# A third place for output weights' parts, filled by adding DMAs two tiles ahead, and more projection steps before attention's first scores

## The chip, the cores and the metric

The kernel runs on one core of a Trainium2 chip. Its metric is the time of one execution on the device in microseconds (us). The time before is the median of three runs, 1197.37 us (1196.95 to 1198.57). One further look comes from the hardware profiler, which recorded one execution instruction by instruction.

Five engines work side by side: TensorE (PE, matmuls; the loading of its weights is listed as PEld), VectorE (DVE), ScalarE (ACT), GpSimd (POOL) and SyncE (SP, which here only issues DMAs). Each works through its own queue in order and waits there for semaphores.

## The reference

One layer of an encoder block on 1024 tokens of width 1024, in float32. The parts that matter here:

```python
n = rmsnorm(h, ln_g)
proj = n @ w_in                       # q, k, v of both head groups
y_na  = neighbourhood_attention(...)  # 8 heads of 64
y_gla = bidirectional_gla(...)        # gated linear attention, 4 heads
h = h + concat([y_na, y_gla]) @ w_out
h = h + square(relu(rmsnorm(h) @ w1)) @ w2
out = rmsnorm(h)
```

All matmuls are made to float32 accuracy from two parts: every operand x is held as a high part (x rounded to the matmul's type) and a low part (x minus the high part). A product takes three matmuls: high by high, high by low, low by high.

## The kernel before, in words

The program is written for a planner. It emits instructions in program order with priorities; the planner fixes the order on each engine, gives tiles their memory and sets the semaphores. A block under `tc.high_priority(offset=n)` is treated as if it had been emitted n places earlier. `tc.keep_in_program_order` fixes an instruction's order among all instructions of its engine that are so marked; all matmuls and transposes are.

**Weights' parts.** `weights(block, eng)` loads a block of 128 by 1024 weights (512 KB) with SP into a tile wf and makes its two parts. With an engine given, `split` lets ACT round wf into wh, and that engine (DVE, called V, or POOL, called G) subtracts: wl = wf - wh. Without one, ACT writes wl = -(wf rounded), POOL issues a DMA which adds the block from memory to wl, and ACT writes wh. wf, wh and wl have two places each in the pool stg: six places of 4 KB per partition, 24 KB in all. The blocks of the input projection go the second way, one block ahead; the blocks of w_out go the first way.

**Attention.** While the attention of one pair of heads runs, the input projection of the next pair fills TensorE's gaps. A list of generators (`Fill`) holds the projections; one step of it is three matmuls (three parts' products for one of eight blocks of the contraction), a half of a block is eight steps, and after each half DVE evacuates the bank. `NA_PRE` steps run before the first scores. Then pairs p = 0 to 3 run over blocks b = 0 to 7; the table `NA_FILL[p][b]` says how many steps stand before the next block's scores (`softmax`), before the current block's turn (`turn`, transposes of the scaled scores) and after it. The projection of a pair's values is followed by transposes of its own, which are held back until `NA_LATE` further steps have run, or until they are needed. `softmax` uses the two banks "s": two products per head, then DVE adds the bias (L804), ACT takes the exponential (L806), DVE scales (L809). `turn` and the value transposes share the two banks "t" (for the last pair's values, "mm"). ACT copies out the high part (L834, L774), DVE subtracts the low one (L835, L775). The first pair's bias is finished by DVE at L749. In pair 3, after block 2, no projection steps are left; from there on the list holds the first half's output tiles.

**Output projection.** The tokens have two halves of 512. For each half there are eight output tiles d of 128 rows; a tile takes 8 blocks of the contraction times three matmuls, 24 in all (`sums`), into a bank "mm", and DVE adds the bank to hT (L716). The first half's tiles run beside the last attention blocks without the last block of the contraction, which follows in eight short products (`opl`) from parts of their own (wk). The second half's tiles (hf = 1) run after it: tile 0, the eight short products, tiles 1 to 7. Each tile's parts are asked for where the tile is emitted, by `split` on DVE for d = 1 to 3 and on POOL for d = 4 to 7. `ff_in` squares each tile on ACT (L932) and sums the squares, on POOL for the first half and on DVE for the second (L934). After tile 2 of the second half, the first half is normed: DVE writes nf (L942), ACT rounds it to n (L947), DVE subtracts (L950).

**Feed-forward.** The pools of the mixer are closed, and the pools mp (ph, pl, uh, ul: three places of 2 KB each, 24 KB in all), mw (raw weights A, four places of 4 KB) and mu take their memory on the left side, from the bottom: mp where stg was, mw over the four tiles yg (4 KB each), mu above. Their tiles wait tile by tile for what lay there. SP loads A (L1021); the first two ph and pl come from `to_two` (L947, L950), then the products u follow.

Of the kernel before, what the change touches and what calls it, by code (L numbers as in the profile page):

```python
# [11 lines left out]
F32R = mybir.dt.float32r  # L12
# [6 lines left out]
P = 128  # L19
D = 1024  # L20
T = 1024
H = 512
NK = D // P
# [27 lines left out]
SOON_W = 100  # L51
SOON_O = 100
SOON_V = 50
NA_PRE = 8
NA_LATE = 4
NA_NEXT = 1
NA_FILL = (
# [9 lines left out]
def block_kernel(ctx, tc, xT, g_mix, w_in, w_z, rpb, na_mask, gu, gb, g_gla, sel_f, sel_b,  # L67
                 rst, w_out, g_ff, w1, w2, g_fin, out):
    nc = tc.nc
    V, S, DMA, G = nc.vector, nc.scalar, nc.sync, nc.gpsimd  # L70

    L = "left"
    R = "right"
    pool = lambda name, side, bufs=1: tc.tile_pool(name=name, bufs=bufs, side=side)
# [7 lines left out]
    stg = stg_stack.enter_context(pool("stg", L, 2))  # L82
    ctx.enter_context(pool("padr", R)).tile([P, 24], F32, tag="padr", name="padr")

    def bank(tag, name):
        return ps.tile([P, H], F32, tag=tag, name=name)
# [36 lines left out]
    class Fill:  # L123
# [5 lines left out]
        def add(self, gen, name=None):  # L129
            self.gens.append((gen, name))  # L130
# [17 lines left out]
        def run(self, steps=1 << 30):  # L148
            while steps > 0 and self.gens:
                steps -= self.step()  # L150
# [10 lines left out]
            while any(t[2] == name for t in self.lates):  # L161
                self.lates.pop(0)[1]()

    def weights(block, eng=None):


        with tc.high_priority(offset=SOON_W):
            wf = stg.tile([P, D], F32, tag="wf", name="wf")
            load = DMA.dma_start(wf, block)
            if eng is not None:  # L170
                return split(wf, eng)
            tc.keep_in_program_order(load)
            wl = stg.tile([P, D], F32R, tag="wl", name="wl")
            tc.keep_in_program_order(S.activation(wl, wf, AF.Copy, scale=-1.0))
            tc.keep_in_program_order(G.dma_start(wl, block, accum_op=ALU.add))
            wh = stg.tile([P, D], F32R, tag="wh", name="wh")
            tc.keep_in_program_order(S.copy(wh, wf))
            return wh, wl

# [11 lines left out]
    def split(wf, eng=None, steps=1):  # L191
        wh = stg.tile([P, D], F32R, tag="wh", name="wh")
        wl = stg.tile([P, D], F32R, tag="wl", name="wl")
        for i in range(steps):
            c = slice(i * D // steps, (i + 1) * D // steps)
            S.copy(wh[:, c], wf[:, c])
            (eng or V).tensor_tensor(wl[:, c], wf[:, c], wh[:, c].bitcast(F32), op=ALU.subtract)
        return wh, wl

    def product(dst, w, xh, xl, ks=range(NK), woff=0, first=True, last=True):  # L200

        wh, wl = w
        for k in ks:
            a = wh[:, woff + k * P: woff + (k + 1) * P]
            b = wl[:, woff + k * P: woff + (k + 1) * P]
            h, l = xh(k), xl(k)
            PE.matmul(dst, a, h, start=first and k == ks[0], stop=False)
            PE.matmul(dst, a, l, start=False, stop=False)
            PE.matmul(dst, b, h, start=False, stop=last and k == ks[-1])
            yield  # L210
# [24 lines left out]
    yg_pool = ctx.enter_context(ExitStack())  # L235
# [14 lines left out]
    def proj(blk, evac):  # L250

        w = block_parts(blk)
        for hf in range(2):
            d = bank("mm", f"proj{blk}_{hf}")
            yield from proj_part(d, w, hf * H, H)
            evac(hf, d)
# [430 lines left out]
    KO = (4, 5, 6, 7, 0, 1, 2, 3)  # L687
# [4 lines left out]
    def to_parts(hf, ks, eng):  # L692
        c = slice(hf * H, (hf + 1) * H)
        t = yhl[hf]
        for k in ks:
            i = KO.index(k)
            S.copy(t[:, i, 0, :], yk(k)[:, c])
            (eng if i % 2 else V).tensor_tensor(t[:, i, 1, :], yk(k)[:, c], t[:, i, 0, :].bitcast(F32), op=ALU.subtract)  # L698

    def out_mm(o, hf, w, ks):  # L700
        t = yhl[hf]
        return product(o, w, lambda k: t[:, KO.index(k), 0, :], lambda k: t[:, KO.index(k), 1, :], ks=ks)

    def sums(hf, d, ks, eng=None, w=None, ahead=()):

        w = w or weights(w_out[d], eng)
        o = bank("mm", f"op{hf}_{d}")
        for i, _ in enumerate(out_mm(o, hf, w, ks)):
            to_parts(hf, ahead[i:i + 1], G)
            yield  # L710
        add(hf, d, o)
# [7 lines left out]
    with soon("na") as ap, soon("qkv") as qp:  # L719
# [20 lines left out]
        def bias_for(p):  # L740


            bt = bt0 if p == 0 else ap.tile([P, 2, 7, P], F32, tag="bt", name=f"bt{p}")
            DMA.dma_start(bt[:, :, 0:3, :], rpb2[:, 2 * p:2 * p + 2, :, :])
            rows = msk[:, 3:4, :].to_broadcast([P, 2, P])
            for i in range(2):
                for o, src, m in ((3, 1, rows), (5, 0, rows), (0, 0, msk[:, 0:3, :])):
                    n = 3 if o == 0 else 2
                    V.scalar_tensor_tensor(bt[:, i, o:o + n, :], bt[:, i, src:src + n, :], 8.0, m,  # L749
                                           op0=ALU.mult, op1=ALU.add)  # L750
            return bt
# [7 lines left out]
        def na_v(p):  # L759
# [18 lines left out]
            def ev(hf, d):  # L778
# [5 lines left out]
                if hf:  # L784
                    fill.later(NA_LATE, transposes, ("v", p))
            return proj(20 + p, ev)

        def softmax(p, b, q, k, bt):

            k0, k1 = max(b - 1, 0), min(b + 1, NB - 1)  # L790
            n = (k1 - k0 + 1) * P
            boff = 384 if b == 0 else 640 if b == NB - 1 else 0
            sc = [bank("s", f"sc{p}_{b}_{i}") for i in range(2)]
            c, kc = slice(b * P, (b + 1) * P), slice(k0 * P, (k1 + 1) * P)
            for i in range(2):
                PE.matmul(sc[i][:, :n], q[i][:, c], k[i][:, kc], start=True, stop=False)
            for i in range(2):
                o = slice(i * 64, (i + 1) * 64)
                PE.matmul(sc[i][:, :n], q[i][o, c], k[2][o, kc], start=False, stop=True)
            sm = ap.tile([P, 2, 3], F32, tag="sm", name="sm", bufs=4)  # L800
            xs = []
            for i in range(2):
                x = ap.tile([P, 384], F32, tag="x", name="xsc", bufs=4)
                V.tensor_tensor_reduce(x[:, :n], sc[i][:, :n], bt.rearrange("p h a b -> p h (a b)")[:, i, boff:boff + n], -0.125, 3.0e38,  # L804
                                       op0=ALU.add, op1=ALU.min, accum_out=sm[:, i, 0:1])
                S.activation(x[:, :n], x[:, :n], AF.Exp, scale=-1.0, bias=sm[:, i, 0:1],  # L806
                             accum_out=sm[:, i, 1:2])
                V.reciprocal(sm[:, i, 2:3], sm[:, i, 1:2])
                V.tensor_scalar(x[:, :n], x[:, :n], sm[:, i, 2:3], None, op0=ALU.mult)  # L809
                xs.append(x)  # L810
            return xs
# [60 lines left out]
        with tc.high_priority(offset=SOON_B):  # L872
            bt = bias_for(0)
        fill.run(NA_PRE)
        xs = softmax(0, 0, *qk, bt)
# [43 lines left out]

    a2 = ctx.enter_context(pool("a2", R))  # L920
    a3 = yg_pool.enter_context(pool("a3", L))
    yp_stack = ExitStack()
    yp = yp_stack.enter_context(pool("op", R, 2))
    n0, acc = half(a2, "n0"), {}

    def ff_in(hf, d):
        c = slice(hf * H, (hf + 1) * H)
        if d == 0:
            acc[hf] = sq = yp.tile([P, H], F32, tag="acc", name=f"acc{hf}")
        else:  # L930
            sq = yp.tile([P, H], F32, tag="sq", name="sq2")
        S.activation(sq, hT[:, d, c], AF.Square)  # L932
        if d:
            (V if hf else G).tensor_tensor(acc[hf], acc[hf], sq, op=ALU.add)  # L934

    def ff_sum(hf):
        v = bank("t", f"v2_{hf}")
        PE.matmul(v, ones, acc[hf], start=True, stop=True)
        return v

    def normed_h(dst, hf, d, r):
        V.scalar_tensor_tensor(dst, hT[:, d, hf * H:(hf + 1) * H], gff[:, d:d + 1], r,  # L942
                               op0=ALU.mult, op1=ALU.mult)
# [17 lines left out]
    wk = split(wf, G)  # L961
    to_parts(0, KO[-1:], V)
    to_parts(1, KO, V)
    run(sums(1, 0, KO, w=w10))
    for d in range(NK):
        o = bank(("t", "s", "o")[d % 3], f"opl_{d}")
        t = yhl[0][:, NK - 1]
        run(product(o, wk, lambda k: t[:, 0, :], lambda k: t[:, 1, :], ks=(0,), woff=d * P))
        add(0, d, o)
        ff_in(0, d)  # L970
    ff_in(1, 0)
    for d in range(1, NK):
        run(sums(1, d, KO, V if d < 4 else G))
        ff_in(1, d)
        if d == 2:
            r0 = rstd_from(ff_sum(0), 1.0 / D, yp, "rs", H, "sq", 2, y=acc[0])
            for k in range(NK):
                nf = yp.tile([P, H], F32, tag="nf", name="nf")
                normed_h(nf, 0, k, r0)
                to_two(n0[:, k, 0, :], n0[:, k, 1, :], nf)  # L980
# [448 lines left out]
    for c0, n in ((H, H), (0, Q), (Q, Q)):  # L1429
# [3 lines left out]
        for d in range(NK):  # L1433
            o = bank("o" if d % 2 else "t", f"f7_{d}_{c0}")[:, :n]
            for k in range(4):
                w = [w7[:, d // 4 * 4 + k, x, d % 4 * P:(d % 4 + 1) * P] for x in range(2)]
# [102 lines left out]
```

## Time and profile before

The profiled execution took 1198.57 us, of which the trace covers 1196.8 us from the first to the last instruction. The table gives, for stretches of the span, the time for which each engine was busy and the clock that TensorE was granted.

| stretch (us) | what runs | PE | DVE | ACT | POOL | clock |
|---|---|---|---|---|---|---|
| 240 to 420 (180.0) | attention of pairs 0 to 2 | 173.12 | 122.82 | 112.06 | 25.44 | 0.98 |
| 420 to 460 (40.0) | pair 3, first output tiles | 38.49 | 32.50 | 25.32 | 11.64 | 1.00 |
| 460 to 489.3 (29.3) | first half's last tiles, second half's tile 0 | 29.30 | 12.80 | 11.64 | 13.06 | 1.00 |
| 489.3 to 495 (5.7) | the short products | 5.70 | 5.39 | 3.66 | 1.47 | 1.00 |
| 495 to 540.5 (45.5) | second half's tiles 1 to 7 | 40.60 | 35.59 | 21.36 | 21.09 | 1.00 |
| 540.5 to 560 (19.5) | first feed-forward products | 19.49 | 10.26 | 10.02 | 0.00 | 0.91 |

How to read what follows. A row of the waits gives an engine and its line, what it waited for, the total in us, how often, and the longest. A row of the timeline gives start, duration (both in us), engine, line, operation, the tiles written and read, their shape and a count of instructions merged into the row; in brackets stands how long the engine had been idle before and what it waited for. A row of the windows gives a stretch, its length, and for each engine the time busy and the number of instructions; then the granted clock, the busy share of the DMA engines and GB/s. A row of the chain gives start, duration and what ran. "Lnnn" is a line of the kernel.

### The profile page before, as it was taken

How to read it: one execution, taken by the hardware profiler on the slowest of the kernel's cores; microseconds unless marked ns; L12 is line 12 of the kernel's file. 1: busy time of each engine (PE TensorE's matmuls, PEld its weight loads, DVE VectorE, ACT ScalarE, POOL GpSimd, SP SyncE). 2: the span in 40 equal slices, each digit the busy share in tenths (PEclk: the TensorE clock that was granted, in tenths of full speed). 3: DMA queues.
4: the chain of work that ended last, by engine and by line, in shares of the span. 5: the costliest groups of instructions: out<-in, count | busy, mean ns of one | idle time of the engine just before them, and what ended most of it. 6: DMA issues, size and time to landing. Idle time of an engine off the chain costs nothing.

```text
span 1196.8 us, 15430 instructions
## 1 busy us (share of the span) xinstructions
PE 1156.5 (97%) x5632; PEld 947.3 (79%) x5632; DVE 873.2 (73%) x1558; ACT 664.8 (56%) x1222; POOL 248.4 (21%) x199
## 2 busy tenths in 40 slices
PE   9999999989999999989999999999999999999995
PEld 8878778767787878867688888888888888888774
DVE  8777867856767786586858885867858768597466
ACT  6867567546666665435634635446355453554654
POOL 5200000202011124530103230402304114041013
PEclk8999999989999999999999999999999999999998
DMA  7333232322323242320210112111211112111204
GB/s 237 75 88 90 43 74 61 75 59 53 77 44 100 67 176 71 106 106 1 85 57 23 57 64 71 36 53 54 71 68 37 54 54 71 54 36 53 71 1 141
DMA packets 40283, 84.03 MB, mean 70 GB/s; under 512 B 9264, under 2 KB 20656, under 8 KB 40208
## 3 DMA queue, kind: packets, MB, share of 16 engines
q1 hardware_dynamic: 36608, 71.11, 17.8%
q0 software_dynamic: 3456, 11.94, 5.8%
q8 instruction: 44, 0.72, 0.2%
q14 instruction: 31, 0.25, 0.1%
q10 hardware_dynamic: 144, 0.00, 0.0%
HBM read 78.85 MB, written 5.96 MB: 71 GB/s over the span
## 4 chain that ended last, share of the span: by engine, by line
PE 76%; DVE 12%; ACT 7%; issue 2%; DMA 1%; POOL 0%; SPq 0%; DVEq 0%; ACTq 0%
PE f L114 24%; PE u L114 21%; PE proj L114 14%; PE op L114 5%; PE sc L114 2%; PE o L114 2%; PE no L114 2%; PE pt L119 1%; PE sb L114 1%; DVE st L595 1%; DVE st L592 1%; PE ob L114 1%; DVE pl L1012 1%; DVE asb L587 1%; DVE nf L942 1%
## 5 line engine op out<-in xcount | busy, mean ns | idle before, releaser
L1034 ACT CAST ph<-A 128x512 fp32r<-128x512 f32 x166 | 103.0, 621 | 146.5 <-PE f L114 73.6
L1012 POOL TENSOR_TENSOR ul<-uB,uh 128x512 fp32r<-128x512 f32 x84 | 109.1, 1317 | 330.5 <-ACT uh L1047 213.4
L114 PE MATMUL f<-uh,ph 128*128 128x512 f32 x400 | 155.8, 390 | 1.5 <-ACT u L1055 1.4
L114 PE MATMUL f<-ul,ph 128*128 128x512 f32 x400 | 155.7, 389 | 0.1
L114 PE MATMUL f<-uh,pl 128*128 128x512 f32 x400 | 155.7, 389 | 0.0
L1012 DVE TENSOR_TENSOR pl<-A,ph 128x512 fp32r<-128x512 f32 x166 | 112.7, 688 | 52.6 <-ACT ph L1034 52.6
L114 PE MATMUL proj<-nh,wh 128*128 128x512 f32 x352 | 150.9, 429 | 0.0
L114 PE MATMUL proj<-nh,wl 128*128 128x512 f32 x352 | 139.2, 396 | 1.2 <-DMA wl<-in_w_in 1.2
L114 PE MATMUL proj<-nl,wh 128*128 128x512 f32 x352 | 138.6, 394 | 0.0
L1194 DVE TENSOR_TENSOR hT<-hT,f 128x512 f32<-128x512 f32 x168 | 113.1, 687 | 19.9 <-PE f L114 19.9
L114 PE MATMUL u<-n,ph 128*128 128x512 f32 x288 | 90.5, 396 | 2.0 <-ACT ph L947 2.0
L114 PEld LDWEIGHTS f<-uh,ph 128*128 128x128 f32 x400 | 75.1, 188 | 17.9 <-ACT u L1055 1.8
L114 PEld LDWEIGHTS f<-ul,ph 128*128 128x128 f32 x400 | 75.1, 188 | 16.0 <-DVE ul L1012 0.4
L114 PEld LDWEIGHTS f<-uh,pl 128*128 128x128 f32 x400 | 75.1, 188 | 15.6
L114 PEld LDWEIGHTS proj<-nh,wh 128*128 128x128 f32 x352 | 67.0, 190 | 18.2 <-issue 5.6
L1047 ACT CAST uh<-uB 128x512 fp32r<-128x512 f32 x84 | 51.9, 618 | 51.0 <-PE f L114 34.2
L114 PEld LDWEIGHTS proj<-nh,wl 128*128 128x128 f32 x352 | 66.6, 189 | 16.7 <-DMA wl<-in_w_in 1.6
L114 PE MATMUL u<-T,ph 128*128 128x512 f32 x256 | 79.2, 391 | 0.1
L114 PEld LDWEIGHTS proj<-nl,wh 128*128 128x128 f32 x352 | 67.1, 191 | 11.8 <-issue 1.7
L114 PE MATMUL op<-y,wh 128*128 128x512 f32 x240 | 75.8, 396 | 0.4 <-DVE y L698 0.4
L114 PE MATMUL u<-nt,ph 128*128 128x512 f32 x224 | 68.9, 389 | 0.0
L806 ACT ACTIVATE xsc<-xsc,sm 128x384 f32<-128x384 f32 (+1 forms) x64 | 37.3, 584 | 52.9 <-DVE sm L804 52.6
(300 smaller groups left out, 2503.2 us busy)
## 6 DMA issues: line engine op xcount, KB each, us to landing
A<-in_w SPq DMA_DIRECT2D x64, 512.0 KB
wf<-in_w_in SPq DMA_DIRECT2D x22, 512.0 KB
wl<-in_w_in POOLq DMA_DIRECT2D x21, 512.0 KB, 6.8
wf<-in_w_out SPq DMA_DIRECT2D x17, 512.0 KB
hT<-in_xT SPq DMA_DIRECT2D x2, 2048.0 KB
xs<-in_xT SPq DMA_DIRECT2D x6, 512.0 KB
out<-hT SPq DMA_DIRECT2D x4, 512.0 KB
out<-hT SPq DMA_DIRECT2D x8, 256.0 KB
```

Of the source, the lines that this page charges most:

```text
L114: m = nc.tensor.matmul(*args, **kw)
L119: tc.keep_in_program_order(nc.tensor.transpose(*args, **kw))
L587: V.copy_predicated(asb[hf], sel.bitcast(U32).to_broadcast([P, 4, P]), src.rearrange("p (a b) -> p a b", a=4))
L592: V.scalar_tensor_tensor(st[0:64, i + 1, :], st[0:64, i, :], dec[0:64, i:i + 1], st[0:64, i + 1, :], op0=ALU.mult, op1=ALU.add)
L595: V.scalar_tensor_tensor(st[64:128, j - 1, :], st[64:128, j, :], dec[64:128, j:j + 1], st[64:128, j - 1, :], op0=ALU.mult, op1=ALU.add)
L806: S.activation(x[:, :n], x[:, :n], AF.Exp, scale=-1.0, bias=sm[:, i, 0:1], accum_out=sm[:, i, 1:2])
L942: V.scalar_tensor_tensor(dst, hT[:, d, hf * H:(hf + 1) * H], gff[:, d:d + 1], r, op0=ALU.mult, op1=ALU.mult)
L1012: return kp(eng.tensor_tensor(l, x, h.bitcast(F32), op=ALU.subtract))
L1034: kp(S.copy(ph, x))
L1047: kp(S.copy(uh, x))
L1194: kp(V.tensor_tensor(hT[:, d, c], hT[:, d, c], o[:, s], op=ALU.add))
```

## The change

Attention: `NA_PRE` grows from 8 to 11 and `NA_LATE` from 4 to 6. Output projection, second half: the parts of tiles 1 to 7 are made in the second way (ACT writes -wf, a DMA issued by POOL adds the block, ACT writes wh). The parts of tiles 1, 4 and 7 get a place of their own, the pool w3 (wl and wh, 8 KB per partition), which lies above a3 and is closed with it; the others stay in stg. Tile 1's parts are asked for before tile 0 is emitted, tile 2's after it, and those of tile d + 2 ahead of tile d.

```diff
-NA_PRE = 8
-NA_LATE = 4
+NA_PRE = 11
+NA_LATE = 6
...
-    def weights(block, eng=None):
+    def weights(block, eng=None, places=None):
...
-            wl = stg.tile([P, D], F32R, tag="wl", name="wl")
+            wl = (places or stg).tile([P, D], F32R, tag="wl", name="wl")
             tc.keep_in_program_order(S.activation(wl, wf, AF.Copy, scale=-1.0))
             tc.keep_in_program_order(G.dma_start(wl, block, accum_op=ALU.add))
-            wh = stg.tile([P, D], F32R, tag="wh", name="wh")
+            wh = (places or stg).tile([P, D], F32R, tag="wh", name="wh")
             tc.keep_in_program_order(S.copy(wh, wf))
             return wh, wl
...
     a3 = yg_pool.enter_context(pool("a3", L))
+    w3 = yg_pool.enter_context(pool("w3", L))
...
     to_parts(1, KO, V)
+
+    out_w = lambda d: weights(w_out[d], places=w3 if d % 3 == 1 else None)
+    w1d = {1: out_w(1)}
     run(sums(1, 0, KO, w=w10))
+    w1d[2] = out_w(2)
     for d in range(NK):
...
     for d in range(1, NK):
-        run(sums(1, d, KO, V if d < 4 else G))
+        if d + 2 < NK:
+            w1d[d + 2] = out_w(d + 2)
+        run(sums(1, d, KO, w=w1d.pop(d)))
         ff_in(1, d)
```

## The prediction

> **What bounds the kernel now.** I read the page's head, then who TensorE waited for, then the granted clock by stretch around those waits, then each engine's timeline there.
>
> ```profile
> span 1196.8 us, 15430 instructions
> ...
> PE op L114 <- POOL wl L197: 2.8, 2, 1.8
> PE sc L114 <- DVE sm L804: 2.6, 2, 2.2
> ...
> PE nvt L119 <- DVE pt L835: 2.4, 2, 1.2
> PE u L114 <- ACT ph L947: 2.0, 1, 2.0
> ```
>
> TensorE sets the time, and the change removes no matmul; it can only win where TensorE waits. Four of its largest waits (total, times, longest) lie where the edits are: the first scores (sc), the value transposes (nvt), output tiles waiting for a weight's low part (op), and the first feed-forward product (u). Together 9.8 us. Two of them are followed by a lower clock:
>
> ```profile
> core 0: us, PE busy (x) PEld busy (x) DVE busy (x) ACT busy (x) POOL busy (x), PEclk, DMA share, GB/s
> ...
> 126.00:130.00 4.00, 2.58 (x17) 2.17 (x17) 2.84 (x9) 1.78 (x4) 0.00 (x0) 0.73 0.77 173
> ...
> 255.00:258.20 3.20, 3.13 (x14) 2.17 (x12) 3.10 (x6) 1.79 (x2) 0.86 (x1) 1.00 0.23 22
> 258.20:262.40 4.20, 1.69 (x5) 0.77 (x5) 2.90 (x10) 1.21 (x4) 0.00 (x0) 0.83 0.96 224
> 262.40:268.00 5.60, 5.60 (x17) 4.04 (x16) 3.32 (x14) 2.05 (x6) 0.00 (x0) 0.52 0.02 7
> ...
> 524.00:533.00 9.00, 6.62 (x27) 4.87 (x28) 8.73 (x11) 3.35 (x5) 3.64 (x3) 1.00 0.18 71
> ...
> 540.50:545.00 4.50, 4.49 (x13) 3.40 (x13) 1.16 (x2) 0.18 (x1) 0.00 (x0) 0.62 0.00 0
> ```
>
> PEclk is the granted clock. From 262.4 it is 0.52 while PE is wholly busy: 5.60 x 0.48 = 2.7 us lost. From 540.5: 4.50 x 0.38 = 1.7 us. So these two waits cost twice, once as idle time and once as clock. Prices of work at full clock:
>
> ```profile
> 249.14 5.50 PE proj L114 x24
> ...
> 470.50 19.07 PE op L114 x84
> ...
> 495.01 10.67 PE op L114 x47
> ```
>
> A projection step (three matmuls) is 5.50/8 = 0.69 us; an output tile (24 matmuls) 24 x 19.07/84 = 5.45 us. The second half's tile 1 starts at 495.01.
>
> **Part A: three steps ahead of the first scores, transposes two steps later.** The step counts of the table stay, so between two attention events the same number of steps stands as before, shifted in content by three. Two places differ: three more steps stand before pair 0's first scores, and three are missing in pair 3, block 2, where the list has run dry. Moved with them: V's two evacuations on DVE and, at each block's end, ACT's two weight copies, POOL's DMA issue and SP's next load, all three steps earlier against attention.
>
> ```profile
> 260.34 0.44 PE L114 MATMUL sc<-k00p,q 128*128 128x384 f32 x1 [2.21 <-DVE sm L804]
> 261.15 0.69 PE L114 MATMUL sc<-k10p,q 128*128 128x384 f32 x1 [0.37 <-DVE sm L804]
> ...
> 254.67 0.69 DVE L783 TENSOR_TENSOR vT<-proj,rms 128x512 f32<-128x512 f32 x1 [1.25 <-PE proj L114]
> ...
> 258.05 1.89 DVE L749 SCALAR_TENSOR_TENSOR bt<-bt,msk 128x256 f32<-128x256 f32 x5
> 259.86 0.42 DVE L804 CUSTOM_DVE_ANT_0 xsc<-sc,bt 128x256 f32<-128x256 f32 x1
> ...
> 262.50 0.56 DVE L804 CUSTOM_DVE_ANT_0 xsc<-sc,bt 128x384 f32<-128x384 f32 x1 [1.40 <-PE sc L114]
> ...
> 263.52 0.35 DVE L809 TENSOR_SCALAR xsc<-xsc,sm 128x256 f32<-128x256 f32 x1
> ```
>
> The second scores wait for a bank that DVE empties at 259.86, because DVE is still at the norm and the bias (busy 3.10 of 3.20 us from 255.0). DVE does not move: the first scores come 2.06 us later, about 256.5, still before 259.86. So PE, which ran dry at 258.1, runs dry at 259.9 + (its four steps end there): the idle 2.21 + 0.37 becomes about 0.45 + 0.37. But only one step, not two-odd, is then left before the first turn, which needs the scaled block (263.52); DVE's order puts that behind the second scores' bias (262.50, which now can start about 0.5 earlier). PE ends that step near 262.6, the scaled blocks come near 263.4 and 263.9: new waits of 0.9 and 0.3. Idle 2.58 becomes 2.0, a gain of 0.6; broken into four pieces over 4 us. I take it that the clock stays up: +2.7. Bounds: DVE scales first, then only 0.8 idle (gain 1.8 + 2.7); or the clock falls all the same (0.6).
>
> ```profile
> 271.05 1.04 ACT L174 ACTIVATE wl<-wf 128x1024 fp32r<-128x1024 f32 x1
> ...
> 272.93 0.84 ACT L834 CAST pt<-pt 128x384 fp32r<-128x384 f32 x2
> ...
> 274.05 1.12 PE L119 MATMUL nvt<-ident,vT 128*128 128x128 f32 x8 [1.18 <-DVE pt L835]
> ```
>
> The value transposes wait for a bank because ACT's two weight copies (271.05 to 272.93) stand ahead of the copy that empties it. Those copies follow V's last step, which now ends three steps earlier, before the turn; so the bank is free some 1.1 us after the turn (272.93 to 274.05, copy and subtraction). Counting steps, the transposes come one step after the turn in pair 0 (two before) and two in pair 1 (three before): waits of about 0.5 (both banks) and 0.2 in place of 2.4. Gain 1.7; bounds 0 (another collision) to 2.4.
>
> ```profile
> 430.00:440.00 10.00, 8.89 (x49) 6.66 (x47) 9.71 (x25) 8.44 (x22) 5.55 (x3) 1.00 0.80 284
> ...
> 432.55 1.44 PE L114 MATMUL no<-pt,vhl 128*128 128x256 f32 x8 [0.96 <-DVE vhl L775]
> ```
>
> In pair 3 the three missing steps were cover: DVE is busy 9.71 of 10 us there and PE already waits 0.96. Their 2.06 us of work is done at the start, but PE cannot use all of the room. Lost between 0 and 2.06; I take 1.5, near the DVE row. **A: 0.6 + 2.7 + 1.7 - 1.5 = 3.5 us.**
>
> **Part B: output weights for the second half.** Seven tiles (1 to 7) change the way in which the low part is made.
>
> ```profile
> L174 ACT ACTIVATE wl<-wf x21: 1042/1059/1068, 46.1 to 395.0; 128x1024 fp32r<-128x1024 f32 x21
> L175 POOL DMA_DIRECT2D wl<-in_w_in x21: 853/862/927, 47.5 to 397.0; - x21
> ...
> DMA to landing us min/median/max: 5.3/6.8/9.3
> ...
> 482.77 16.17 SPq L169 DMA_DIRECT2D wf<-in_w_out  x4
> ...
> 485.50:486.00 0.50, 0.50 (x3) 0.39 (x3) 0.00 (x0) 0.00 (x0) 0.50 (x1) 1.00 0.18 74
> ...
> 528.78 1.04 ACT L196 CAST wh<-wf 128x1024 fp32r<-128x1024 f32 x1
> ...
> 529.90 2.44 POOL L197 TENSOR_TENSOR wl<-wf,wh 128x1024 fp32r<-128x1024 f32 x1 [5.36 <-ACT wh L196]
> ...
> 532.40 0.50 PE L114 MATMUL op<-y,wl 128*128 128x512 f32 x1 [1.79 <-POOL wl L197]
> ```
>
> Removed: four POOL subtractions (2.44 each) and three of DVE, for tiles 1 to 3. Added: seven ACT copies (7.4 us), seven POOL issues (6.0) and seven adding DMAs of 512 KB. All lies beside matmuls; what counts is the chain per tile. Before: place freed, ACT copy (held up on ACT behind the casts of n), POOL 2.4, then PE: late by 1.0 and 1.79, the op wait above. Now: place freed (a tile later there are two tiles left, 10.9 us), copy 1.06, issue, landing 6.8: 8 us, slack 2.9. At the slowest landing, 9.3, slack is 0.4; ACT held up by one n cast then costs a little. I take 0.4 us of the 2.8 as coming back, the median row being nearest, bounds 0 to 2.8. The new wait is ACT's, for the place; behind it on ACT stand squares and casts of n, and behind POOL's issue the sums of squares; PE asks for these only at the norm and at u, after the tiles. Tile 1 has less room: its load, asked for at 482.77, moves until about 486 (the DMA share falls to 0.18), the copy ends near 487.1, and POOL, busy at 485.5 with a subtraction of 2.44, issues by 487.9: landing 494.7, needed near 495.5. **B1: 2.4 us.**
>
> ```profile
> 517.87 1.93 SPq L1021 DMA_DIRECT2D A<-in_w  x4
> ...
> 538.50 0.63 ACT L932 ACTIVATE sq<-hT 128x512 f32<-128x512 f32 x1 [4.28 <-DVE hT L716]
> 539.03 1.12 ACT L947 CAST ph<-A 128x512 fp32r<-128x512 f32 x2
> ...
> 539.69 0.74 PE L114 MATMUL u<-n,ph 128*128 128x512 f32 x2 [2.01 <-ACT ph L947]
> ```
>
> The feed-forward's raw weights (A) are requested at 517.87, yet ACT, idle 4.28 us, casts the first only behind the last square. By the code, ph lies in pool mp, 24 KB per partition, exactly over stg (six places of 4 KB), and the last tile's parts occupy stg until its last matmul; A lies over other, long finished tiles. With tile 7 in the third place, stg is done one tile (5.45 us) earlier, and ph and pl (0.6 and 0.7 us each) fit before the tile ends. So 2.0 idle and the 1.7 of clock go. SP's loads of wf run earlier too (a place of wf is then freed by ACT's copies, not by POOL's subtraction), so A, behind them in SP's queue, comes no later. Bounds: 0 to 3.7; I take 3.7. **B: 2.4 + 3.7 = 6.1 us.**
>
> What is late next: the norm of the second half, which hangs on the last tile's sum and so moves along.
>
> **Sum:** 3.5 + 6.1 = 9.6 us. The profiled execution took 1198.57 (span 1196.8 and 1.8 around it), so its like is 1189.0; it lay 1.2 above the median 1197.37, from which I take 1187.8.
>
> **Rivals.**
>
> *The clock falls at the first scores anyway* (2.0 us idle in pieces; at 126 us 1.4 of idle in pieces sufficed for 0.73, while 1.79 in one piece at 532 left 1.00): 9.6 - 2.7, so 1190.5. Chance 0.14.
>
> *ph stays behind the last square*: for it, its place in ACT's order is the planner's; against, the memory argument. 9.6 - 3.7: 1191.5. Chance 0.13.
>
> *Clock not tied to these gaps*: both drops stay, 9.6 - 4.4 = 5.2: 1192.2. Chance 0.06, as both drops begin right behind a gap. The Trainium skill, "TensorE: Matmul & The Clock Gate", section "Why this matters for your kernels", speaks for this one: it warns only of gaps over about 3 us. The trace disagrees: 2.21 and 2.01 sufficed.
>
> *ACT hands over late as now*: tile 7's cast stands at 528.78, and tile 5 ended near 532.40 - 1.79 - 0.45 - 1.0 - 5.45 = 523.7, so 5.1 us after its place was free. 5.1 + 1.06 + 6.8 = 13.0 is 2.1 over two tiles; with 1.0 at tile 6, as now, and 1.7 of clock behind such a gap, 4.8 us are lost in place of 0.4: 9.6 - 4.4 = 5.2, 1192.2. Against: parts asked for two tiles ahead stand earlier in ACT's order than the casts that hold them up now. Chance 0.09. Together with the ph rival the gain is 1.5: 1195.9; chance of such pairs 0.12.
>
> *Slower: POOL's order.*
>
> ```profile
> 493.45 10.38 POOL L934 TENSOR_TENSOR acc<-acc,sq 128x512 f32<-128x512 f32 x7 [5.96 <-ACT sq L932]
> ```
>
> If tile 2's DMA issue (input ready about 492) is queued behind all seven sums of squares, it goes out at 503.8 and lands at 510.6, where tile 2 is due at 500.4: 10.2 us lost and some 2 of clock: 9.6 - 12.2, so 1200.0. It decides from the point where more than one sum stands ahead (1.48 each, slack about 2). Against: higher priority and input ready first. Chance 0.08.
>
> **How the numbers follow.** Forecast 0.38; with the better ends of the unknown costs (1.2 at the first turn, 0.7 at the transposes, 1.5 in pair 3, 0.4 in B1) it gains 3.8 more, 1184.0. Faster by over 0.2% (2.4 us, about what can be told from no change): 0.38 + 0.14 + 0.13 + 0.06 + 0.09 = 0.80; within: the pairs, 0.12; slower: 0.08. The range from 1184.0 to 1194.5, 2.3 beyond the rivals at 1192.2 for the worse ends, holds those 0.80.
>
> **What would show it.** Right: sc idle near 0.8 and no clock of 0.5 near 262; nvt waits under 1; no wait of op for wl from 495 on, the tile chain near 38 us; ph cast before the last square, PE going from op to u without a gap at full clock. Wrong: op waiting for a DMA, 1 us or more of new waits in pair 3 beyond 1.5, or POOL issues behind acc.

## The result, and the profile after

The changed kernel takes 1218.38 us (median of 4 runs, 1217.06 to 1220.94), the kernel before, run beside it, 1197.58. The ratio is 1.0177, with a 95% interval of 1.0163 to 1.0192: 20.8 us slower, where 9.6 us less were forecast. The profiled execution took 1217.06 us. Its short products start at 493.64 us (before: 489.40), and its first feed-forward product at 558.96 (before: 539.69). So attention lost 4.2 us, the second half's output tiles lost 19.3 - 4.2 = 15.0, and little was lost or won elsewhere. The two profiled executions differ by 18.5 us, so 2.3 of the 20.8 us between the medians are not in these traces.

The page's head, and the rows of who TensorE waited for (total, times, longest), of the changed kernel:

```profile
span 1215.3 us, 15440 instructions
...
PE op L114 <- ACT wh L177: 7.3, 1, 7.3
PE op L114 <- DMA wl<-in_w_out: 7.1, 3, 4.9
PE no L114 <- ACT pt L834: 5.9, 4, 2.2
PE u L114 <- ACT ph L948: 2.0, 1, 2.0
PE no L114 <- DVE vhl L775: 1.6, 1, 1.6
PE pt L119 <- DVE pt L835: 1.4, 2, 1.1
...
PE sc L114 <- DVE sm L804: 0.5, 2, 0.4
PE nvt L119 <- DVE pt L835: 0.4, 2, 0.2
```

The waits that part A was to shorten are shorter: the first scores (sc) 0.5 in place of 2.6, the value transposes (nvt) 0.4 in place of 2.4. But the value products (no) now wait 5.9 us for ACT's copy of pt (the transposed scores), a wait that the page before does not have. Output tiles (op) wait 7.3 + 7.1 = 14.4 us in place of 2.8. The wait of u for ph is still there, to the hundredth.

The granted clock in the stretches around these waits, same kernel (stretch, its length, busy time and count on PE, PEld, DVE, ACT, POOL, then the clock, DMA share and GB/s):

```profile
262.40:268.00 5.60, 4.95 (x18) 3.52 (x16) 3.45 (x15) 3.94 (x8) 0.86 (x1) 0.70 0.08 18
...
525.00:532.30 7.30, 0.04 (x1) 0.04 (x1) 6.02 (x10) 5.06 (x8) 0.73 (x1) 0.84 0.00 0
532.30:539.00 6.70, 1.83 (x4) 1.01 (x5) 0.00 (x0) 2.17 (x3) 1.00 (x2) 0.50 0.91 216
539.00:544.00 5.00, 5.00 (x14) 3.91 (x13) 0.00 (x0) 1.62 (x2) 3.40 (x3) 0.54 1.02 315
```

Behind the two long waits TensorE runs at half clock: 1.83 x 0.50 + 5.00 x 0.46 = 3.2 us. With 14.4 - 2.8 = 11.6 us more of waiting that makes 14.8 of the 15.0 us.

The timeline of the output stage shows who is late. Start, duration, engine, line, operation, and in brackets the idle time before it and what ended it:

```profile
508.19 1.04 ACT L174 ACTIVATE wl<-wf 128x1024 fp32r<-128x1024 f32 x1
...
517.42 1.28 ACT L948 CAST n<-nf 128x512 fp32r<-128x512 f32 x2 [2.34 <-DVE nf L943]
...
529.04 1.28 ACT L948 CAST n<-nf 128x512 fp32r<-128x512 f32 x2 [1.85 <-DVE nf L943]
530.23 1.05 ACT L174 ACTIVATE wl<-wf 128x1024 fp32r<-128x1024 f32 x1
...
532.12 1.05 ACT L174 ACTIVATE wl<-wf 128x1024 fp32r<-128x1024 f32 x1
...
538.63 1.06 ACT L174 ACTIVATE wl<-wf 128x1024 fp32r<-128x1024 f32 x1 [4.53 <-DMA wf<-in_w_out]
...
505.69 26.88 SPq L169 DMA_DIRECT2D wf<-in_w_out  x3
...
532.26 1.22 PE L114 MATMUL op<-y,wh 128*128 128x512 f32 x2 [7.27 <-ACT wh L177]
...
538.35 0.80 PE L114 MATMUL op<-y,wl 128*128 128x512 f32 x1 [4.87 <-DMA wl<-in_w_out]
```

The copy at 508.19 is tile 4's. Tile 5's comes at 530.23, behind all eight casts of n, though tile 2, whose place it takes, ended near 511. ACT is not short of time between 517 and 529: it is idle before nearly every cast, waiting for DVE's nf, and the copy stands behind these waits. When it comes, PE has been dry for some 5 us. Tile 6's copy follows at once; SP's next load waits 26.88 us for a place of wf that ACT did not give back, so tile 7's raw block arrives only at 538.6.

In attention, a similar picture where pair 1 gives way to pair 2, same kernel and view:

```profile
361.26 1.06 ACT L174 ACTIVATE wl<-wf 128x1024 fp32r<-128x1024 f32 x1
362.23 1.03 ACT L177 CAST wh<-wf 128x1024 fp32r<-128x1024 f32 x1
363.28 0.43 ACT L834 CAST pt<-pt 128x128 fp32r<-128x128 f32 x2
...
363.60 1.12 PE L114 MATMUL no<-pt,vhl 128*128 128x384 f32 x4 [2.19 <-ACT pt L834]
```

ACT's two weight copies, moved three steps earlier, stand ahead of the copy of pt that PE needs next. So do three casts of pair 2's keys (L419, L421), which fill ACT from 359.35 to 361.24, right up to the copies; the theory below leaves these out.

### The profile page after: what moved, and what is told of

Read it like the earlier page. It is cut to its first block, busy times and chain, and to the rows that moved or that the text cites. A ratio compares the mean times of both kernels' runs of the same rounds, so it can differ in the third digit from the quotient of the medians.

```text
span 1215.3 us, 15440 instructions
## 1 busy us (share of the span) xinstructions
PE 1159.5 (95%) x5632; PEld 947.7 (78%) x5632; DVE 861.3 (71%) x1555; ACT 670.4 (55%) x1229; POOL 243.9 (20%) x202
## 4 chain that ended last, share of the span: by engine, by line
PE 75%; DVE 11%; ACT 7%; issue 4%; DMA 2%; SPq 0%; DVEq 0%; ACTq 0%; POOLq 0%
PE f L114 24%; PE u L114 21%; PE proj L114 13%; PE op L114 6%; PE no L114 2%; PE o L114 2%; PE sc L114 1%; DMA wl<-in_w_out 1%; PE pt L119 1%; PE sb L114 1%; DVE st L595 1%; DVE st L592 1%; PE ob L114 1%; DVE pl L1019 1%; DVE asb L587 1%
## 5 line engine op out<-in xcount | busy, mean ns | idle before, releaser
L114 PEld LDWEIGHTS u<-n,ph 128*128 128x128 f32 x288 | 54.5, 189 | 14.3 <-ACT ph L948 2.4
```

The source lines that it names most:

```text
L114: m = nc.tensor.matmul(*args, **kw)
```

## Experiments

The theory after this reading: both losses are ACT's order. In the output stage the copies of tiles 5 to 7 stand behind the casts of n because they are asked for behind the norm. In attention the moved weight copies stand ahead of pt's copies. The main rival in the output stage is that adding DMAs are too slow for two tiles, by POOL's queue or by their landing. (In the expectations of e3 and e11, the two small waits are put at tiles 3 and 4; by the timeline they stand at tiles 2 and 3.) "Before" in this section is the kernel before, run beside each group: 1198.36, 1197.72 and 1197.81 us (e1 to e4, e5 to e8, e9 to e12).

### e1 and e2: each part alone

```diff
 e1, against the kernel before
-NA_PRE = 8
-NA_LATE = 4
+NA_PRE = 11
+NA_LATE = 6
 e2, against the changed kernel
-NA_PRE = 11
-NA_LATE = 6
+NA_PRE = 8
+NA_LATE = 4
```

> The kernel before with the two attention constants alone (11 and 6). Theory (ACT's two weight copies, now three steps earlier, stand ahead of the copies of pt that the value products wait for; DVE fuller in pair 3): the attention stage keeps all of the loss that the changed kernel shows there, 4.2 us, so about 1201.8 us; 'no' waits for pt near 5 us in all, and the op waits from 495 on are the old ones (1.0 and 1.8). Rival (the attention of the changed kernel was disturbed only through the new memory pool and order): 1194 to 1197 us, no waits of 'no' for pt.

> The changed kernel with the attention constants of before (8 and 4). Theory (the output stage loses by itself): attention as before, op waits of about 7 for ACT's wh and about 5 for the DMA of wl, and a lower clock behind them: 15 us over before, about 1212.5 us. Rival (the two parts work on each other, the attention part's 4 us being in both): within 3 us of the changed kernel's 1218, or below 1207.

e1: 1202.63 us, ratio 1.0035 (1.0022 to 1.0048), so +4.3 us. e2: 1211.79 us, ratio 1.0115 (1.0100 to 1.0130), so +13.4 us. Both parts lose by themselves, each about what the traces gave it. The two sum to 17.7 us, the changed kernel's loss is 20.8: the 3 us between are about as much as the intervals allow, and no run shows whether they have a source. The new attention waits of e1 (no for pt and for vhl, the parts of the values; pt for DVE's pt) are word for word the three rows of the changed kernel above: 5.9, 1.6 and 1.4 us. The third place and the DMAs have no part in them.

### e3 and e4: where tile 5's copy stands

```diff
 e3, against e2
-        if d + 2 < NK:
+        if d + 2 < NK and d != 3:
             w1d[d + 2] = out_w(d + 2)
         run(sums(1, d, KO, w=w1d.pop(d)))
         ff_in(1, d)
         if d == 2:
+            w1d[5] = out_w(5)
             r0 = rstd_from(...)
 e4, against e2
-            tc.keep_in_program_order(S.activation(wl, wf, AF.Copy, scale=-1.0))
+            S.activation(wl, wf, AF.Copy, scale=-1.0)
...
-            tc.keep_in_program_order(S.copy(wh, wf))
+            S.copy(wh, wf)
```

> e2 with one step moved: tile 5's parts are asked for right after tile 2's squares, ahead of the norm of the first half, not behind it. Theory (ACT's order: the copies of tiles 5 to 7 stand behind all eight casts of n because they are asked for behind the norm's block): the waits of 7.3 and 4.9 and the clock below 1 behind them go, only the 1.9 and 0.4 at tiles 3 and 4 stay, about 1197 us (1195 to 1199). Rival (the adding DMAs, their issues in POOL's queue and their landing of 8.5 us, are too slow for two tiles): op keeps waits of 5 us and more for the DMA of wl, 1206 us or more.

> e2 with the fixed program order taken off ACT's two copies, so that the planner places them by priority. It places tile 5's ahead of the norm, tile 6's ahead of the casts of n and tile 7's behind four of them; wh of tiles 3 to 6 comes ahead of wl, 1 us later for the DMA. Theory (ACT's order): as e3, at most 2 us worse for the later DMAs, 1196 to 1201 us. Rival (slow adding DMAs): 1206 us or more.

e3: 1197.32 us, ratio 0.9990 (0.9981 to 1.0000). e4: 1194.72 us, ratio 0.9971 (0.9960 to 0.9982). Asking for one tile's parts a few lines earlier wins back 14.5 us; the number, place and size of the adding DMAs are the same. ACT's timeline in e3, the copies of tiles 5, 6 and 7 and the first cast between them, and the one row of op that is left in its waits:

```profile
508.81 1.04 ACT L174 ACTIVATE wl<-wf 128x1024 fp32r<-128x1024 f32 x1
...
517.15 1.04 ACT L174 ACTIVATE wl<-wf 128x1024 fp32r<-128x1024 f32 x1
...
519.04 1.13 ACT L948 CAST n<-nf 128x512 fp32r<-128x512 f32 x2
...
522.81 1.04 ACT L174 ACTIVATE wl<-wf 128x1024 fp32r<-128x1024 f32 x1
```

```profile
PE op L114 <- DMA wl<-in_w_out: 2.2, 2, 1.8
```

With this the rival falls: the same DMAs, landing after a median of 8.0 us (8.4 in e2), cost 2.2 us once the copy ahead of them is in time. e4 says the same in another way: without the marks, the planner itself puts the copies of tiles 5 and 6 ahead of the casts, and tile 7's between them. It came out faster than expected, and its gain over e3 lies before the short products, which start at 482.79 us there, 7.0 us earlier than in e3 (that execution, 1191.77 us, is the fastest of ten, so the trace overstates the gain); e6 follows that up.

Why the planner put tile 5's copy behind all eight casts is not shown. Being asked for behind the norm is not enough: in e3 the parts of tiles 6 and 7 are asked for behind it too, and their copies stand ahead of the first cast (517.15) and between the casts (522.81). What e2, e3 and e4 show is that the place in ACT's order was the cause of the loss.

### e5 and e9: the two constants apart

```diff
 e5, against the kernel before
-NA_LATE = 4
+NA_LATE = 6
 e9, against the kernel before
-NA_PRE = 8
+NA_PRE = 11
```

> The kernel before with the transposes' delay alone (6; the first constant stays 8). Theory (the harm of e1 comes from the weight copies moved three steps ahead, which the first constant does): the copies stay where they were, the transposes come two steps later and find their banks: nvt waits fall from 2.4 to under 1, no new waits of 'no' for pt, 1196.5 us (1195 to 1198). Rival (the later transposes do the harm: the value parts come later, and no waits for vhl): 1200 us or more.

> The kernel before with 11 in place of 8 steps ahead of the first scores; the transposes keep their delay of 4. Theory (the moved steps alone do the harm: the weight copies ahead of pt's copies, DVE fuller in pair 3): at least as slow as e1, 1202 to 1206 us, with the 'no' waits for pt of e1. Rival (it takes both constants together): 1199 us or less.

e5: 1195.06 us, ratio 0.9977 (0.9964 to 0.9990), 2.7 us faster. e9: 1206.40 us, ratio 1.0075 (1.0062 to 1.0089), 8.6 us slower. So the later transposes were right, and the three steps ahead of the first scores do the harm. The waits of e9:

```profile
PE no L114 <- ACT pt L834: 5.9, 4, 2.2
...
PE pt L119 <- DVE vhl L775: 2.3, 2, 1.5
...
PE no L114 <- DVE vhl L775: 1.6, 1, 1.6
PE pt L119 <- DVE pt L835: 1.4, 2, 1.1
PE nvt L119 <- DVE pt L835: 1.2, 1, 1.2
```

The first wait is e1's. The second is new: transposes of pt waiting for DVE's vhl (L775), which empties the same banks; e1, with the longer delay, does not have it.

### e6 and e7: is it the two weight copies?

```diff
 e6, against the kernel before
-            tc.keep_in_program_order(S.activation(wl, wf, AF.Copy, scale=-1.0))
+            S.activation(wl, wf, AF.Copy, scale=-1.0)
...
-            tc.keep_in_program_order(S.copy(wh, wf))
+            S.copy(wh, wf)
 e7, against e6
-NA_PRE = 8
-NA_LATE = 4
+NA_PRE = 11
+NA_LATE = 6
```

> The kernel before with the program order taken off ACT's two weight copies, attention constants and output weights as before. e4 came to its short products 6.3 us earlier than the kernel before. Theory (it is the copies' order against the copies of pt, in attention, that e4 gained by): nvt waits go, 1193.5 us (1191 to 1196). Rival (e4 gained by the output stage's new order): 1197 to 1199 us.

> e6 with the attention constants 11 and 6. Theory (the loss of e1 is the weight copies ahead of pt's copies; unmarked, the planner puts them elsewhere): the 'no' waits for pt fall from 5 us to under 2, and it lies at most 1 us over e6. Rival (the moved steps cost by themselves, in DVE's order and in pair 3): the loss of e1 stays, 4 us over e6.

e6: 1192.65 us, ratio 0.9951 (0.9931 to 0.9970), 5.1 us faster than the kernel before; nvt is gone from its waits. That is about half of the gain: the first scores already start at 257.62 us, 2.7 us earlier than in the kernel before (260.34), so the other half lies ahead of this attention, which the theory did not count on. e7: 1197.44 us, ratio 0.9992 (0.9983 to 1.0002), 4.8 us over e6. Here the theory misses: it had given e7 at most 1 us over e6, and the rival, 4 us over e6, came true. The waits of e7:

```profile
PE no L114 <- ACT pt L834: 2.9, 4, 1.8
...
PE no L114 <- DVE pt L835: 1.2, 2, 0.6
```

The wait for pt has halved, so the fixed place of the weight copies caused about half of it; the time lost is no smaller for that (4.8 us here, 4.3 in e1). The longest wait left, 1.76 us at 391.23, has other instructions of ACT right ahead of it:

```profile
389.65 0.60 ACT L419 CAST qap<-qt 64x512 fp32r<-64x512 f32 x1
390.27 0.61 ACT L419 CAST qbp<-qt 64x512 fp32r<-64x512 f32 x1
390.91 0.43 ACT L834 CAST pt<-pt 128x128 fp32r<-128x128 f32 x2
```

These are the casts of the next pair's q, made when its projection is evacuated. They were moved three steps earlier too. So the weight copies are not the whole cause; other work that the moved steps hand to ACT stands ahead of pt's copies as well. How the 4.8 us divide between these casts, DVE's fuller order in pair 3 and the clock was not separated.

### e8: the first casts of the feed-forward's weights

The last tile's square is put behind the first two casts of ph, and the subtractions for these two low parts go from DVE to POOL:

```diff
     def ff_in(hf, d, kept=False):
...
+        c = S.activation(sq, hT[:, d, c], AF.Square)
+        if kept:
+            tc.keep_in_program_order(c)
...
-        ff_in(1, d)
+        if d < NK - 1:
+            ff_in(1, d)
...
-            to_two(ph, pl, f1.w.t[...][:, 0:H])
+            to_two(ph, pl, f1.w.t[...][:, 0:H], eng=G, kept=True)
             f1.parts[p, i] = ph, pl
+    ff_in(1, NK - 1, kept=True)
```

> The kernel before with the last tile's square put behind the first two casts of ph in ACT's order, and the low parts pl of these two on POOL. Nothing else is moved, and the parts of tile 7 stay where they were. Theory (ph was late by its place in ACT's order alone): the wait of u for ph, 2.0, goes, and with it the low clock behind it (1.7): 1194.6 us (1193.5 to 1196). First rival (memory, the prediction's argument: ph lies over the last tile's parts and waits for them): ph starts only when tile 7 is done, 1198 us. Second rival (the clock falls there anyway): 1196.4 us.

e8: 1195.02 us, ratio 0.9976 (0.9967 to 0.9986), 2.7 us faster. Its timeline and a stretch behind it:

```profile
533.36 0.63 ACT L932 ACTIVATE sq<-hT 128x512 f32<-128x512 f32 x1 [3.23 <-DVE hT L716]
533.89 1.13 ACT L949 CAST ph<-A 128x512 fp32r<-128x512 f32 x2
...
537.29 0.62 PE L114 MATMUL u<-n,ph 128*128 128x512 f32 x2
...
538.27 0.63 ACT L932 ACTIVATE sq<-hT 128x512 f32<-128x512 f32 x1 [3.25 <-DVE hT L716]
```

```profile
540.00:545.00 5.00, 4.56 (x18) 3.31 (x18) 2.88 (x3) 3.20 (x6) 1.68 (x2) 1.00 0.00 0
```

ph is cast at 533.89, while tile 7 is computed from parts in the old place. So memory did not hold it: the planner had put it behind the last square. PE goes from op to u without a wait, and the clock stays at 1.00, where it was 0.62 in the trace before. The median gains 1.0 less than 2.0 + 1.7. A wait of 0.44 for the sum of squares that comes up right behind (4.56 busy of 5.00 above) is a part of that; another is probably that the low clock does not follow this gap in every execution (last section).

### e10, e11 and e12: repairs together, and POOL's order

e10 is the changed kernel with 8 steps ahead of the first scores, e3's order and e8's order; it keeps the later transposes, the third place and the adding DMAs. e11 moves the first half's sums of squares from POOL to DVE:

```diff
-            (V if hf else G).tensor_tensor(acc[hf], acc[hf], sq, op=ALU.add)
+            V.tensor_tensor(acc[hf], acc[hf], sq, op=ALU.add)
```

e12 is the kernel before with the edits of e5, e6 and e8, and its output weights as they were.

> The changed kernel with three repairs: 8 steps ahead of the first scores (the transposes keep 6), tile 5's parts asked for ahead of the norm (e3), the last square behind the first two ph (e8). If the three work at different places, their gains add up: 1198 - 2.7 (e5) - 1.0 (e3) - 2.7 (e8) = 1191.6 us (1190 to 1193.5). If they share one (the clock, the norm), 1194 us or more.

> e10 with the first half's sums of squares on DVE, not on POOL. Theory (tile 3's adding DMA is late because its issue stands behind these sums in POOL's queue): the op waits for the DMA of wl at tiles 3 and 4 (1.8 and 0.5) go, 2 us below e10. Rival (the DMA is late by its own landing time): the waits stay, as e10; if the sums delay the norm on DVE, slower than e10.

> The kernel before with unmarked weight copies (e6), transposes' delay 6 (e5) and ph ahead of the last square (e8); output weights as before. e5 and e6 both take the nvt waits away, so of e5 little is added to e6: 1192.6 - 2.7 - (0 to 1) = 1189.5 us (1188 to 1191). If the unmarked copies' gain lay in the clock only: 1192 us or more.

e10: 1191.43 us, ratio 0.9951 (0.9939 to 0.9964). e11: 1189.00 us, ratio 0.9928 (0.9914 to 0.9941). e12: 1189.19 us, ratio 0.9931 (0.9918 to 0.9943). The three gains add up as expected. POOL's timeline in the changed kernel shows what e11 takes away (with ACT's copy of tile 3 and PE's wait for it):

```profile
499.06 6.79 POOL L935 TENSOR_TENSOR acc<-acc,sq 128x512 f32<-128x512 f32 x5 [0.91 <-ACT sq L933]
...
503.68 1.04 ACT L174 ACTIVATE wl<-wf 128x1024 fp32r<-128x1024 f32 x1
...
506.33 2.67 POOL L935 TENSOR_TENSOR acc<-acc,sq 128x512 f32<-128x512 f32 x2 [0.48 <-ACT sq L933]
508.94 1.77 POOL L175 DMA_DIRECT2D wl<-in_w_out  x2
...
514.28 0.50 PE L114 MATMUL op<-y,wl 128*128 128x512 f32 x1 [1.88 <-DMA wl<-in_w_out]
```

The copy is done at 504.7, the issue goes out at 508.9, behind all seven sums. In e11 no sum stands there, and tile 3's wait is gone. What is left is 0.3 at tile 2, whose issue had no sum ahead of it in the changed kernel either, so the expectation that both waits go holds for one of them:

```profile
PE op L114 <- DMA wl<-in_w_out: 0.3, 1, 0.3
```

## Why the prediction was wrong

The prediction gave 1187.8 us, in a range of 1184.0 to 1194.5; the kernel takes 1218.38. Step by step:

*First scores.* Right in the waits: 2.58 became 0.17 + 0.38 at the scores and 0.65 at the turn, 1.2 us, a little better than the 2.0 forecast. The clock is not settled by one trace: from 262.4 on it was granted 0.70 in place of 0.52, so 4.95 x 0.30 = 1.5 us stay lost of the 2.7 that were to be won. But e1, e7 and e9, with the same three waits to within 0.02 us, have 1.00 in the matching stretch. This is e1's row:

```profile
262.40:268.00 5.60, 4.89 (x23) 3.38 (x22) 4.19 (x18) 4.21 (x9) 0.86 (x1) 1.00 0.15 22
```

So the step (the clock stays up) held in three of the four traces that have these waits, and its rival in one.

*Value transposes.* Right: 2.4 became 0.4, and alone (e5) the longer delay gains 2.7 us, in an interval of 1.2 to 4.3 that holds the 1.7 forecast.

*The moved steps.* **Here the first step fails.** The prediction listed what moves with them, ACT's weight copies among it, and gave it no price: only pair 0's start and pair 3's end were counted, since "between two attention events the same number of steps stands as before". The number is the same, but the evacuation after each half, and with it ACT's casts and weight copies, stands at another place between the events. Of this came 5.9 us of waiting for pt's copy and, outside pair 3, 1.1 + 0.2 for its low part (at 289.18 and 309.05): 7.2, where part A was to gain 0.6 + 2.7 + 1.7 = 5.0. Pair 3, which had been priced at 1.5, cost less in waits: in the changed kernel (at 433.59, 436.60 and 438.51) they are 0.33 + 1.62 + 0.64 = 2.6, against 0.5 + 1.0 + 0.4 = 1.9 before.

*Output weights, B1.* **The step that cost most** is the sentence "parts asked for two tiles ahead stand earlier in ACT's order than the casts that hold them up now". Tile 5's parts are asked for ahead of tile 3, but that is behind the norm of the first half, whose eight casts are emitted after tile 2; its copy came behind all eight. The mechanism had been named as a rival at 0.09 (ACT hands over late as now), and priced from tile 7 of the kernel before, with 5.1 us from the place's end to its cast; at tile 5 it is 530.23 - 511 = 19 us. Its price was 4.8 us; it was 7.3 + 4.9 of waits and 3.2 of clock. The chain itself was priced within 2 us: the seven DMAs of the output weights landed after

```profile
DMA to landing us min/median/max: 5.3/8.5/9.8
```

in place of a median of 6.8 and a slowest of 9.3, and e11, where copy and issue are in time, waits 0.3 us in all.

*POOL's order.* The slower rival happens, but at tile 3 and not at tile 2, with 4.2 us of delay at the issue and 1.9 us at PE, not 10.2.

*First feed-forward product, B2.* This step fails too: freeing stg one tile earlier was to let ph go ahead, and won nothing (2.0 of wait before and after). Most of the gain forecast is there to be had (2.7 of 3.7, e8), but not by the change: ph did not wait for memory, it stood behind the last square in ACT's order. The rival had it right. The 1.7 of clock in the term was one execution's: behind the same gap it was lost in half of the traces (last section).

The forecast size of what these places hold was not far off: with ACT's and POOL's orders mended, and only the later transposes kept of part A, the same third place and DMAs run in 1189.00 us (e11). That it comes this near is partly chance: e11 wins nothing at the first scores, whose wait of 2.6 stays, and its repair at ph is not in the change. Nor is it owed to the adding DMAs alone: e12, with the old output weights and unmarked copies, is as fast.

## What to carry to other kernels

Asking early is not running early: on an engine that works its queue in order, look up what is emitted between the request and its use, and count the waits of those instructions, not only their busy time. When filler work is moved against a chain, price every instruction that it hands to other engines, at each place where it lands anew, not only where the filler runs out. A wait that stays the same to the hundredth after its supposed cause is gone, as u's did here, may be a matter of order; one mark on one instruction tests it.

## What was not expected of the hardware

How far a gap of TensorE lowers the clock does not follow from the gap's length. In e10 the wait for tile 3's DMA is 2.32 us, longer than the two gaps of 2.21 and 2.01 on which the prediction built, and the clock behind it stays whole:

```profile
508.94 0.50 PE L114 MATMUL op<-y,wl 128*128 128x512 f32 x1 [2.32 <-DMA wl<-in_w_out]
```

```profile
508.90:512.00 3.10, 3.06 (x13) 2.55 (x14) 0.69 (x1) 2.26 (x4) 0.00 (x0) 1.00 0.99 211
```

The same gap goes both ways. The wait of 2.01 us before u stands in ten of the fourteen traces. In five of them (before, changed, e3, e4, e9) the clock of the 4.5 us that begin 0.8 us after it is 0.62 or 0.69; in the other five (e1, e2, e5, e6, e7) it is 1.00. e1:

```profile
545.55 0.73 PE L114 MATMUL u<-n,ph 128*128 128x512 f32 x2 [2.01 <-ACT ph L947]
...
546.36:550.86 4.50, 4.49 (x18) 3.37 (x19) 1.16 (x2) 1.20 (x3) 0.00 (x0) 1.00 0.00 0
```

Where the gap is gone (e8, e10, e11, e12), the clock stays at 1.00. That fits the gap being a cause, but four traces are few against five of ten that stay up with it. The gap of 2.2 us at the first scores is firmer: it stands in ten traces, mostly with 0.37 more behind it, and over the 5.6 us that begin 2 us after it the clock is 0.50 to 0.78 in all ten. So a clock loss read from one execution is not a fixed price of its gap.

The Trainium skill, "TensorE: Matmul & The Clock Gate", Part 1, says that the activity is judged in windows of about 3.4 us that run freely, so that the phase counts. That agrees with gaps of one length going both ways; that a whole idle window is needed does not agree, since 2.01 us was followed by a low clock in five traces.
